# Attention scores over all 128 partitions: q's two parts stacked, k's parts copied to both halves by transfers

## The chip, the cores and the metric

The kernel runs on one core of one Trainium2 chip. The metric is device time in microseconds (us) of one execution. The engines are named as in the profile: PE (TensorE matmul), PEld (its weight load), DVE (VectorE), ACT (ScalarE), POOL (GpSimd) and SP (SyncE).

## What is computed

Two blocks of a small transformer, one after the other, on 512 tokens of width 1024, all in float32. The first block has two attentions of 8 heads with head width 64: a windowed one in which four query heads share a key head (call it a), and a neighbourhood one in which every head has keys of its own (b). The second block is run for two layers, each with one sliding-window attention (c) between two feed-forward parts. What matters here are the scores, cut from the reference:

```python
# a: windowed_gqa, 128 queries against up to 3 blocks of 128 keys
sc = jnp.einsum('bqkgd,bskd->bkgqs', qi, ki).astype(jnp.float32) * scale
# b: neighborhood_attn
sc = jnp.einsum('bchd,brckhd->bhcrk', qr, kn).astype(jnp.float32) * scale
# c: sliding_window_attention, 128 queries against 2 blocks of 128 keys
scores = jnp.einsum("bnqkgd,bnskd->bnkgqs", qb, k_band).astype(jnp.float32) * scale
p = jnp.exp(scores - m)
```

`d` is the head width of 64, so a score sums over 64 products. The rest of each block is matrix products of the whole 512 x 1024 activation with weights of 234 MB in all.

## The kernel before

Every float32 matrix is split into an upper part (the value rounded to the short float32 that PE multiplies in one pass, type fp32r) and a lower part (what is left over). A product is three matmuls: upper times upper, upper times lower, lower times upper (`Tile.mm`, L450 to L452, 128 x 512 each). ACT makes the upper part and DVE the lower one, for weights (`split_item`, L376 and L378, tiles `wh` and `wl`) as for activations (`split_act`, L553 and L554). Split activations live in 52 slots, tiles `r`, that are taken and given back (`take`, `give`). SP loads the weights from a stream in program order.

A tile of q or k holds two heads, one on partitions 0 to 63 and one on partitions 64 to 127. When its product is done, `ev_split` takes it out of PSUM: DVE multiplies by the norm's factor (tile `evs`), ACT writes the upper part into one slot, DVE the lower part into another. A head's q and k then lie on the same 64 partitions.

`run_attention` goes through steps of 128 queries and two heads: 32 steps in the first block (16 of a, tiles `sa`, then 16 of b, tiles `sb`) and 16 in each layer of the second (tiles `sc`). Four steps share a q tile; in b each four steps have a k tile of their own, in a and c one k tile serves all. A step `s` is four functions: `qk` (scores on PE at L717, then bias and row maximum on DVE), `soft` (exponential on ACT, division on DVE), `tr` (PE transposes the probabilities, `pt`) and `pv_` (times v, `yp`). `tr` runs one step behind `qk` in the first block and two steps behind in the second, `pv_` another step behind. Between these, fillers keep PE at work: other projections of the same block, in an order written out by hand (`FILL_AB`, `FILL_C`), each cut in parts of `STEP` = 2 row blocks, paced so that they last through all steps. Before step 0, `2 * head` such parts are done. The q and k tiles of later steps are fillers too; the last k tile of b, `("kb", 3)`, is followed by `("vb", 3)`, and then comes step 12 of b, which needs both. Queues run in order on each engine, so a `qk` that waits holds up all of PE behind it.

The head of each attention is `linear2`: q's and k's products side by side, then v's, in the midst of which q and k are taken out.

POOL does little: some additions at the very start, twelve loads of b's bias (L992, tile `bb`) and eight reloads of x (L1037). An `ft` tile is one of five buffers for passing values such as `evs`.

Of the kernel before, what the change touches and what calls it, by code (L numbers as in the profile page):

```python
# [15 lines left out]
P = 128  # L16
# [215 lines left out]
def two_blocks(ctx, tc, plan, xT, wstream, vecs, sinks, rpb_g, dists, masks, outT):  # L232
# [464 lines left out]
    def make_attention(kind, q, k, v, y, bias_of, sink_idx, band):  # L697
# [6 lines left out]
        def qk(s):  # L704
            c, i = divmod(s, 4)
            ks = keys(i)
            n = P * len(ks)
            sp = bank(f"s{kind}{s}", True).rearrange("p (g k) -> p g k", g=2)
            qh, ql = q(c)
            kh, kl = k(c)  # L710
            w = max(n, 2 * P)
            sl = slice(P * ks[0], P * ks[0] + w)
            for g in range(2):
                r = slice(HD * g, HD * g + HD)
                qs = slice(P * i, P * i + P)
                for j, (a, b) in enumerate(((qh, kh), (qh, kl), (ql, kh))):
                    nc.tensor.matmul(sp[:, g, :w], a[r, qs], b[r, sl], start=(j == 0), stop=(j == 2))  # L717
            bt = bias_of(c, i)
            t = big("t", f"t{kind}{s}").rearrange("p (g k) -> p g k", g=2)
            mx = sm_p.tile([P, 8], F32, tag="mx", name=f"mx{kind}{s}")  # L720
            for g in range(2):
                nc.vector.tensor_tensor_reduce(
                    out=t[:, g, :n], in0=sp[:, g, :n], in1=bt[:, g, :n], scale=1.0, scalar=-3.0e38,
                    op0=ALU.add, op1=ALU.max, accum_out=mx[:, g:g + 1])
            nm = mx[:, 2:4]
            if sink_idx is None:
                nc.vector.tensor_scalar(nm, mx[:, 0:2], -1.0, None, ALU.mult)
            else:
                sv = snk[:, sink_idx, :].rearrange("p (g c) -> p c g", g=2)[:, c, :]
                nsv = nsnk[:, sink_idx, :].rearrange("p (g c) -> p c g", g=2)[:, c, :]  # L730
                nc.vector.scalar_tensor_tensor(nm, mx[:, 0:2], -1.0, nsv, ALU.mult, ALU.min)
                nc.vector.tensor_tensor(mx[:, 4:6], nm, sv, ALU.add)
            state[s] = (t, mx, n, ks)
# [50 lines left out]

        return qk, soft, tr, pv_

    def run_attention(steps, fillers, needs, head=1, late=False):

        n = len(steps)
        lag = LAG2 if late else LAG1  # L790
        slots = n + lag + 1
        hold = [] if late else [50, 51]
        assert all(i in free for i in hold)
        free[:] = [i for i in free if i not in hold]
        total = sum(f[1] for f in fillers)
        parts, have, cost = [], set(), [0.0]
        queue = list(fillers)

        def fill():
            if not parts:  # L800
                key, c, make = queue.pop(0)
                fs = make()
                parts.extend((key if i == len(fs) - 1 else None, c / len(fs), f) for i, f in enumerate(fs))
            key, c, f = parts.pop(0)
            cost[0] += c
            f()
            have.add(key)

        def fill_to(share, slack):
            while (queue or parts) and cost[0] < total * share - slack:  # L810
                fill()

        for _ in range(2 * head):
            fill()
        total -= cost[0]
        cost[0] = 0.0

        for s in range(slots):
            if s < n:
                while not set(needs(s)) <= have:  # L820
                    fill()
                if any(key[-len(k):] == k for k in needs(s) for key, _ in evacs):
                    evacuate()
                steps[s][0](steps[s][4])
            evacuate()
            fill_to((s + MID) / slots, SLACK[0])
            if s > lag:
                k = s - lag - 1
                steps[k][3](steps[k][4])
            if lag <= s < n + lag:  # L830
                steps[s - lag][2](steps[s - lag][4])
            if s < n:
                rest = steps[s][1](steps[s][4])
                split_to(st["next"] + 2)
                rest()
            fill_to((s + 1) / slots, SLACK[1])
        assert not queue and not parts
        evacuate()
        flush()
        give(hold)  # L840
# [15 lines left out]
            inv.rearrange("p (r c) -> p r c", r=8), ALU.mult, ALU.mult)  # L856
        return t

    def ev_split(ids, scale=1.0, turn=scaled):
        def f(ps):  # L860
            split_act(turn(ps, "evs", scale), slot[ids[0]], slot[ids[1]])
        return f

    def ev_v(ids, turn=scaled):
# [68 lines left out]
    nc.vector.tensor_tensor(gfg, vcols(("norm_final", None)), vcols(("ffn1_norm_2", 0)), ALU.mult)  # L933
    nc.vector.tensor_scalar(nsnk, snk, -1.0, None, ALU.mult)
    qa, ya, yb, qb, kb, vb = {0: take(2)}, {}, {}, {}, {}, {}
    ka, va = take(2), take(2)
    linear2(MIX1_HEAD, xop, [ev_split(qa[0], QS), ev_split(ka), ev_v(va)], ar, KC, make_inv)
    ya_done = []

    def ev_ga(n):  # L940
# [17 lines left out]
    def fill(key):  # L958
        def make():
            if key[0] == "ga":  # L960
                return halves(key, xop, ev_ga(key[1]))
            if key[0] == "gb":
                return halves(key, xop, ev_gb(key[1]))
            if key[0] == "pa":
                assert ya_done
                return halves(key, [pair_of(ya[k]) for k in range(4)], ev_pa(key[1]))
            ids = take(2)
            {"qa": qa, "qb": qb, "kb": kb, "vb": vb}[key[0]][key[1]] = ids
            ev = {"qa": lambda: ev_split(ids, QS), "qb": lambda: ev_split(ids, QS, scaled_by_columns),
                  "kb": lambda: ev_split(ids, 1.0, scaled_by_columns), "vb": lambda: ev_v(ids, scaled_by_columns)}  # L970
            return halves(key, xop, ev[key[0]]())
        return (key, 0.5 if key[0] == "pa" else 1.0, make)

# [21 lines left out]
    def rpb_bias(c, i):  # L995
# [9 lines left out]
        if i != 2:  # L1005
            nv = (c, v + 1) if v < 2 else (c + 1, 0)
            if nv[0] < 4 and nv not in bias_cache:
                rpb_load(*nv)
        return bt[:, :, P:] if i == 0 else bt

    f_a = make_attention("a", ids_pair(qa), lambda c: pair_of(ka), lambda c: pair_of(va),
                         y_plain(ya, lambda c: qa[c] + (ka + va if c == 3 else []), ya_done),
                         alibi("a", 0, 384), 0, (-1, 0, 1))
    f_b = make_attention("b", ids_pair(qb), ids_pair(kb), ids_pair(vb),
                         y_plain(yb, lambda c: qb[c] + kb[c] + vb[c]), rpb_bias, None, (-1, 0, 1))

    def needs_ab(s):
# [291 lines left out]

    def mix2(l, before):  # L1310
        qs, ys, tmp = {0: take(2)}, {}, {}
        ks, vs = take(2), take(2)
        linear2([(l,) + k for k in MIX2_HEAD], xop, [ev_split(qs[0], QS), ev_split(ks), ev_v(vs)], ar, 1, make_inv)
        cs = [take(2, late=True) for _ in range(4)]
        nc.vector.tensor_tensor(inv2, inv, inv, ALU.mult)

# [22 lines left out]
        def fl(key):  # L1339
            def make():  # L1340
                if key[0] == "q":
                    qs[key[1]] = take(2)
                    return halves((l,) + key, xop, ev_split(qs[key[1]], QS))
                return halves((l,) + key, xop, ev_conv(*key))
            return (key, 1.0, make)

        f_c = make_attention(f"c{l}", ids_pair(qs), lambda c: pair_of(ks), lambda c: pair_of(vs),
                             y_plain(ys, lambda c: qs[c] + (ks + vs if c == 3 else [])),
                             alibi(f"c{l}", 384, 256), 1 + l, (-1, 0))
        run_attention([(*f_c, s) for s in range(16)], [fl(k) for k in FILL_C],  # L1350
# [80 lines left out]
```

## Time and profile before

| what | value |
|---|---|
| median of 3 runs | 2463.43 us (2463.13 to 2463.51) |
| the profiled execution: device time | 2464.76 us |
| its span on the core | 2463.0 us |
| granted PE clock, mean | 0.996 |
| PE busy | 2436.1 us, 99% |
| DVE busy | 1960.7 us, 80% |
| ACT busy | 1261.0 us, 51% |
| POOL busy | 24.6 us, 1% |

The profiled execution took 1.33 us more than the median of the runs. An engine's busy time is the time in which at least one of its instructions is under way; matmuls overlap each other, so a share of 99% says that PE had nothing to wait for, not that it could do no more.

### The profile page before, as it was taken

To read this page: it belongs to the slowest core of one execution; us is meant where nothing else is said; L and a number is where in the kernel's file an instruction comes from. 1 tells how busy PE (TensorE), PEld (TensorE's weight loads), DVE (VectorE), ACT (ScalarE), POOL (GpSimd) and SP (SyncE) were. 2 spreads that over 40 slices of the span, in tenths; PEclk is the share of its full clock that TensorE was granted. 3 is DMA by queue.
4 is the path that set the end of the run, shared out by engine and by line. 5 is a ranking of instruction groups with operands and counts; after the bars stand their busy time and mean duration, and the time that the engine had idled before them with its cause. 6 is when DMAs were issued, how large, how long until landed. Compare 5 with 4: busy or idle time off the path is not lost.

```text
span 2463.0 us, 39488 instructions
## 1 busy us (share of the span) xinstructions
PE 2436.1 (99%) x15098; PEld 2167.0 (88%) x15098; DVE 1960.7 (80%) x3943; ACT 1261.0 (51%) x2744; POOL 24.6 (1%) x37
## 2 busy tenths in 40 slices
PE   8999999999999999999999999999999999999998
PEld 6888888999879999988899999899999878999997
DVE  7778678877679878768798888898887687988885
ACT  5554355544455545544565445665445455654454
POOL 2000000000000000000000000000000000000000
PEclk9999999999999999999999999999999999999999
DMA  4222432233322332332223323323333322233332
GB/s 161 69 92 88 118 114 82 94 101 100 106 85 91 101 115 88 114 95 69 84 80 103 107 99 101 102 93 112 98 104 106 102 69 77 75 107 108 106 94 79
DMA packets 73901, 239.45 MB, mean 97 GB/s; under 512 B 8320, under 2 KB 10384, under 8 KB 73712
## 3 DMA queue, kind: packets, MB, share of 16 engines
q1 hardware_dynamic: 70496, 228.10, 29.0%
q0 software_dynamic: 1776, 7.27, 1.0%
q8 instruction: 118, 1.93, 0.3%
q10 hardware_dynamic: 1440, 1.57, 0.2%
q14 instruction: 71, 0.58, 0.1%
HBM read 234.81 MB, written 2.10 MB: 96 GB/s over the span
## 4 chain that ended last, share of the span: by engine, by line
PE 93%; DVE 5%; ACT 1%; issue 0%; DMA 0%; SPq 0%; DVEq 0%; ACTq 0%
PE X L1084 7%; PE X L1083 7%; PE X L1082 7%; PE YZ L1082 5%; PE YZ L1083 5%; PE YZ L1084 5%; PE mlp_D L451 2%; PE mlp_D L450 2%; PE mlp_D L452 2%; PE 0, 'ffn2'_D L450 2%; PE 1, 'ffn1'_D L450 2%; PE 0, 'ffn1'_D L450 2%; PE 0, 'ffn1'_D L451 2%; PE 0, 'ffn2'_D L451 2%; PE 1, 'ffn1'_D L451 2%; PE 0, 'ffn1'_D L452 2%
## 5 line engine op out<-in xcount | busy, mean ns | idle before, releaser
L378 DVE TENSOR_TENSOR wl<-raw,wh 128x512 fp32r<-128x512 f32 (+2 forms) x890 | 531.7, 609 | 98.3 <-ACT wh L376 91.4
L376 ACT CAST wh<-raw 128x512 fp32r<-128x512 f32 (+2 forms) x890 | 469.6, 555 | 8.4 <-DMA raw<-in_w 2.6
L1082 PE MATMUL X<-r,wh 128*128 128x256 f32 x1568 | 445.2, 284 | 3.8 <-ACT g L1088 3.6
L1084 PE MATMUL X<-r,wl 128*128 128x256 f32 x1568 | 444.0, 283 | 0.0
L1083 PE MATMUL X<-r,wh 128*128 128x256 f32 x1568 | 443.9, 283 | 0.0
L376 ACT CAST wh<-s 128x512 fp32r<-128x512 f32 x392 | 242.7, 620 | 224.6 <-DVE s L355 219.2
L1082 PE MATMUL YZ<-r,wh 128*128 128x256 f32 x1176 | 334.4, 284 | 0.8 <-ACT u L1094 0.8
L1083 PE MATMUL YZ<-r,wh 128*128 128x256 f32 x1176 | 333.3, 283 | 0.0
L1084 PE MATMUL YZ<-r,wl 128*128 128x256 f32 x1176 | 333.2, 283 | 0.0
L378 DVE TENSOR_TENSOR wl<-s,wh 128x512 fp32r<-128x512 f32 x392 | 268.8, 686 | 69.5 <-ACT wh L376 67.6
L1082 PEld LDWEIGHTS X<-r,wh 128*128 128x128 f32 x1568 | 300.1, 191 | 15.2 <-ACT g L1088 4.0
L1083 PEld LDWEIGHTS X<-r,wh 128*128 128x128 f32 x1568 | 300.1, 191 | 10.3 <-issue 1.2
L1084 PEld LDWEIGHTS X<-r,wl 128*128 128x128 f32 x1568 | 300.2, 191 | 0.0
L1082 PEld LDWEIGHTS YZ<-r,wh 128*128 128x128 f32 x1176 | 226.3, 192 | 1.6 <-ACT u L1094 1.4
L1083 PEld LDWEIGHTS YZ<-r,wh 128*128 128x128 f32 x1176 | 226.3, 192 | 0.2 <-issue 0.2
L1084 PEld LDWEIGHTS YZ<-r,wl 128*128 128x128 f32 x1176 | 226.3, 192 | 0.0
L1096 ACT COPY g<-X 128x256 f32<-128x256 f32 x98 | 36.5, 372 | 141.6 <-PE X L1084 141.5
L1097 DVE TENSOR_TENSOR u<-u,g 128x256 f32<-128x256 f32 x98 | 41.6, 424 | 75.8 <-ACT g L1096 75.8
L450 PE MATMUL mlp_D<-r,wh 128*128 128x512 f32 x256 | 100.1, 391 | 0.0
L451 PE MATMUL mlp_D<-r,wh 128*128 128x512 f32 x256 | 100.1, 391 | 0.0
L452 PE MATMUL mlp_D<-r,wl 128*128 128x512 f32 x256 | 99.6, 389 | 0.0
L1092 ACT COPY u<-X 128x256 f32<-128x256 f32 x98 | 36.5, 373 | 101.0 <-PE X L1084 101.0
(429 smaller groups left out, 5258.9 us busy)
## 6 DMA issues: line engine op xcount, KB each, us to landing
raw<-in_w SPq DMA_DIRECT2D x320, 512.0 KB, 3.7
raw<-in_w SPq DMA_DIRECT2D x64, 384.0 KB, 3.5
raw<-in_w SPq DMA_DIRECT2D x32, 448.0 KB, 3.5
raw<-in_w SPq DMA_DIRECT2D x32, 320.0 KB, 2.9
raw<-in_w SPq DMA_DIRECT2D x28, 256.0 KB, 2.6
bb<-in_rpb POOLq DMA_DIRECT2D x12, 384.0 KB, 3.3
xt<-in_x POOLq DMA_DIRECT2D x8, 256.0 KB, 2.9
xt<-in_x SPq DMA_DIRECT2D x1, 1024.0 KB, 12.7
```

What stands on the lines that cost most here:

```text
L376: nc.scalar.copy(h[:, :w], src)
L378: nc.vector.tensor_tensor(lo[:, :w], src, h[:, :w].bitcast(F32), ALU.subtract)
L450: nc.tensor.matmul(self.ps, h[:, c], hx, start=(self.n == 1), stop=False)
L451: nc.tensor.matmul(self.ps, h[:, c], lx, start=False, stop=False)
L452: nc.tensor.matmul(self.ps, lo[:, c], hx, start=False, stop=end)
L1082: nc.tensor.matmul(out, h[:, c], hx, start=first, stop=False, skip_group_check=skip)
L1083: nc.tensor.matmul(out, h[:, c], lx, start=False, stop=False, skip_group_check=skip)
L1084: nc.tensor.matmul(out, l[:, c], hx, start=False, stop=(k == 3), skip_group_check=skip)
L1092: nc.scalar.copy(u[:, lo], out)
L1096: nc.scalar.copy(g[:, hi], out)
L1097: nc.vector.tensor_tensor(u[:, hi], u[:, hi], g[:, hi], ALU.add)
```

## The change

`ev_split` is replaced by `ev_q` and `ev_k`. Both take the product out of PSUM as before (DVE, then ACT for the upper part into an `ft` tile `evh`, then DVE for the lower part, now in place in `evs`). Then POOL issues copies from SBUF to SBUF of 64 partitions x 512 columns each. For q there are four: each head gets a slot of its own, with the upper part on one half of the partitions and the lower part on the other. For k there are eight: each head gets two slots, one with its upper part on both halves, one with its lower part on both halves. `qk` then does two matmuls for a head instead of three, each over 128 partitions: the stacked q against the doubled upper part of k, and against the doubled lower part. This also adds the product of lower and lower part, which was left out before. k takes four slots instead of two, and `head` goes from 1 to 2.

```diff
             sp = bank(f"s{kind}{s}", True).rearrange("p (g k) -> p g k", g=2)
-            qh, ql = q(c)
-            kh, kl = k(c)
             w = max(n, 2 * P)
             sl = slice(P * ks[0], P * ks[0] + w)
             for g in range(2):
-                r = slice(HD * g, HD * g + HD)
-                qs = slice(P * i, P * i + P)
-                for j, (a, b) in enumerate(((qh, kh), (qh, kl), (ql, kh))):
-                    nc.tensor.matmul(sp[:, g, :w], a[r, qs], b[r, sl], start=(j == 0), stop=(j == 2))
+                qg, kg = slot[q(c)[g]], k(c)[2 * g:2 * g + 2]
+                for j in range(2):
+                    nc.tensor.matmul(sp[:, g, :w], qg[:, P * i:P * i + P], slot[kg[j]][:, sl], start=(j == 0), stop=(j == 1))
...
-    def run_attention(steps, fillers, needs, head=1, late=False):
+    def run_attention(steps, fillers, needs, head=2, late=False):
...
-    def ev_split(ids, scale=1.0, turn=scaled):
+    def parts(ps, scale, turn):
+
+        t = turn(ps, "evs", scale)
+        h = ft("evh")
+        split_act(t, h.bitcast(F32R), t)
+        return h, t
+
+    def move(i, half, src, head):
+        nc.gpsimd.dma_start(slot[i].bitcast(F32)[HD * half:HD * half + HD, :], src[HD * head:HD * head + HD, :])
+
+    def ev_q(ids, turn=scaled):
+
         def f(ps):
-            split_act(turn(ps, "evs", scale), slot[ids[0]], slot[ids[1]])
+            h, lo = parts(ps, QS, turn)
+            for src, flip in ((h, 0), (lo, 1)):
+                for g in range(2):
+                    move(ids[g], g ^ flip, src, g)
+        return f
+
+    def ev_k(ids, turn=scaled):
+
+        def f(ps):
+            for j, src in enumerate(parts(ps, 1.0, turn)):
+                for g in range(2):
+                    for half in range(2):
+                        move(ids[2 * g + j], half, src, g)
         return f
...
-    ka, va = take(2), take(2)
-    linear2(MIX1_HEAD, xop, [ev_split(qa[0], QS), ev_split(ka), ev_v(va)], ar, KC, make_inv)
+    ka, va = take(4), take(2)
+    linear2(MIX1_HEAD, xop, [ev_q(qa[0]), ev_k(ka), ev_v(va)], ar, KC, make_inv)
...
-        ks, vs = take(2), take(2)
-        linear2([(l,) + k for k in MIX2_HEAD], xop, [ev_split(qs[0], QS), ev_split(ks), ev_v(vs)], ar, 1, make_inv)
+        ks, vs = take(4), take(2)
+        linear2([(l,) + k for k in MIX2_HEAD], xop, [ev_q(qs[0]), ev_k(ks), ev_v(vs)], ar, 1, make_inv)
```

Where it moves instructions, first on PE at step 12 of b (its score tile is `sb_2425` before and `sb_2454` after; `vb` is the filler ahead of it). Before:

```order
L451 MATMUL vb_2384<-r_103,wh_2212 128x512
L452 MATMUL vb_2384<-r_102,wl_2213 128x512
L717 MATMUL sb_2425<-r_106,r_112 128x256
L717 MATMUL sb_2425<-r_107,r_112 128x256
L717 MATMUL sb_2425<-r_106,r_113 128x256
```

The same three follow once more, for the head on the other 64 partitions. Now:

```order
L451 MATMUL vb_2404<-r_103,wh_2231 128x512
L452 MATMUL vb_2404<-r_102,wl_2232 128x512
L714 MATMUL sb_2454<-r_114,r_112 128x256
L714 MATMUL sb_2454<-r_115,r_112 128x256
L714 MATMUL sb_2454<-r_118,r_113 128x256
L714 MATMUL sb_2454<-r_119,r_113 128x256
L775 MATMUL yb_2468<-r_138,r_110 128x256
```

Six matmuls became four, at the same place behind `vb`; the fourth reads the slot that k's last two copies fill (`r_119`).

Second, POOL's queue over the same stretch of the program. Before it holds bias loads only:

```order
L992 DMA bb_2040<-in_rpb 128x768
L992 DMA bb_2136<-in_rpb 128x768
L992 DMA bb_2203<-in_rpb 128x768
L992 DMA bb_2333<-in_rpb 128x768
L992 DMA bb_2434<-in_rpb 128x768
```

Now the copies stand among them (`x2` is two of a kind in a row; the four `r_112` and `r_113` are q's for steps 12 to 15 of b, the eight behind `bb_2363` are k's for the same steps):

```order
L1012 DMA bb_2222<-in_rpb 128x768
L864 DMA r_112<-evh 64x512
L864 DMA r_113<-evh 64x512
L864 DMA r_112<-evs 64x512
L864 DMA r_113<-evs 64x512
L1012 DMA bb_2363<-in_rpb 128x768
L864 DMA r_114<-evh 64x512 x2
L864 DMA r_118<-evh 64x512 x2
L864 DMA r_115<-evs 64x512 x2
L864 DMA r_119<-evs 64x512 x2
L1012 DMA bb_2461<-in_rpb 128x768
```

Over the whole program POOL gets 64 copies for 16 q tiles and 56 for 7 k tiles.

Third, PE at the first step of a, in the head of the first block. Before, the scores come when half of the filler `qa` is done:

```order
L450 MATMUL qa_373<-r_94,wh_253 128x512
L451 MATMUL qa_373<-r_95,wh_253 128x512
L452 MATMUL qa_373<-r_94,wl_254 128x512
L717 MATMUL sa_392<-r_106,r_104 128x256
L717 MATMUL sa_392<-r_107,r_104 128x256
L717 MATMUL sa_392<-r_106,r_105 128x256
```

Now, with `head` = 2, they come when all of it is done, twelve matmuls and v's four transposes (`vtr`) later:

```order
L452 MATMUL qa_387<-r_102,wl_317 128x512
L891 MATMUL vtr<-ident,evv 128x128 x4
L714 MATMUL sa_429<-r_106,r_104 128x256
L714 MATMUL sa_429<-r_107,r_104 128x256
L714 MATMUL sa_429<-r_108,r_105 128x256
L714 MATMUL sa_429<-r_109,r_105 128x256
L450 MATMUL qa_452<-r_88,wh_322 128x512
```

The first step of c in each layer moves in the same way.

## Rows read from the trace of the kernel before

**Rows 1.** The page: busy time by engine, share of the span, instructions.

```profile
PE 2436.1 (99%) x15098; PEld 2167.0 (88%) x15098; DVE 1960.7 (80%) x3943; ACT 1261.0 (51%) x2744; POOL 24.6 (1%) x37
```

**Rows 2.** Busy time by stretch, around c's first layer: PE, PEld, DVE, ACT, POOL.

```profile
1075.00:1150.00 75.00, 75.00 (x401) 59.32 (x400) 57.52 (x175) 36.33 (x103) 0.00 (x0) 1.00 0.22 66
```

**Rows 3.** Line 717, the scores of b: duration ns min/median/max, first and last start, forms.

```profile
L717 PE MATMUL sb<-r,r x96: 271/333/442, 142.0 to 249.1; 64*128 64x256 f32 x48, 64*128 64x384 f32 x48
```

**Rows 4.** PE in order of time, two score blocks: start us, us, operation, count.

```profile
149.50 0.39 PE L452 MATMUL kb<-r,wl 128*128 128x512 f32 x1
...
150.88 0.39 PE L451 MATMUL kb<-r,wh 128*128 128x512 f32 x1
...
1101.59 0.39 PE L452 MATMUL 0_ch<-r,wl 128*128 128x512 f32 x1
1101.91 0.62 PE L717 MATMUL sc<-r,r 64*128 64x256 f32 x6
1102.47 0.50 PE L450 MATMUL 0_ch<-r,wh 128*128 128x512 f32 x1
1102.81 0.40 PE L451 MATMUL 0_ch<-r,wh 128*128 128x512 f32 x1
```

**Rows 5.** PE in order of time, matmuls over 128 partitions, then transposes.

```profile
1109.45 0.39 PE L452 MATMUL 0_q<-r,wl 128*128 128x512 f32 x1
1109.67 0.88 PE L778 MATMUL yc<-r,r 128*128 128x256 f32 x6
1110.39 0.60 PE L758 MATMUL ptc<-ident,tc 128*128 128x128 f32 x4
1110.75 0.48 PE L450 MATMUL 0_q<-r,wh 128*128 128x512 f32 x1
```

**Rows 6.** PE in order of time, what runs between 1101.80 and 1102.00.

```profile
1101.91 0.39 PE L717 MATMUL sc<-r,r 64*128 64x256 f32 x2
```

**Rows 7.** POOL issuing one load; DMA issues: KB each, median us to landing.

```profile
222.06 0.54 POOL L992 DMA_DIRECT2D bb<-in_rpb  x1 [5.92 <-DVE mxb L727]
...
bb<-in_rpb POOLq DMA_DIRECT2D x12, 384.0 KB, 3.3
xt<-in_x POOLq DMA_DIRECT2D x8, 256.0 KB, 2.9
```

**Rows 8.** ACT and PE in order of time around step 12 of b.

```profile
229.19 0.62 ACT L553 CAST r<-evs 128x512 fp32r<-128x512 f32 x1 [1.99 <-DVE evs L854]
...
229.06 0.39 PE L451 MATMUL vb<-r,wh 128*128 128x512 f32 x1
229.29 0.39 PE L452 MATMUL vb<-r,wl 128*128 128x512 f32 x1
...
231.14 0.39 PE L778 MATMUL yb<-r,r 128*128 128x256 f32 x1
```

**Rows 9.** ACT and PE in order of time around step 8 of b.

```profile
194.73 0.62 ACT L553 CAST r<-evs 128x512 fp32r<-128x512 f32 x1 [3.65 <-DVE evs L854]
...
200.45 0.39 PE L452 MATMUL vb<-r,wl 128*128 128x512 f32 x1
```

**Rows 10.** ACT and PE in order of time around the first step of c.

```profile
1083.82 0.62 ACT L553 CAST r<-evs 128x512 fp32r<-128x512 f32 x1 [1.36 <-DVE evs L846]
...
1086.24 0.39 PE L452 MATMUL 0_q<-r,wl 128*128 128x512 f32 x1
```

**Rows 11.** Busy time by stretch; behind POOL stands the granted clock.

```profile
710.73:714.17 3.44, 0.00 (x0) 0.00 (x0) 3.15 (x6) 3.02 (x6) 0.00 (x0) 1.00 0.83 297
714.17:720.99 6.82, 6.22 (x15) 4.87 (x16) 6.44 (x11) 5.33 (x12) 0.00 (x0) 0.50 0.01 4
751.30:754.18 2.88, 0.04 (x2) 0.00 (x1) 2.88 (x7) 1.46 (x4) 0.00 (x0) 1.00 0.00 0
755.13:758.54 3.41, 3.41 (x19) 3.41 (x17) 3.41 (x7) 0.92 (x4) 0.00 (x0) 0.50 0.02 5
```

**Rows 12.** DVE's waits in the first stage of c: us in total, times, longest.

```profile
DVE tc L722 <- PE sc L717: 0.2, 1, 0.2
```

More of the change, by code (lines that the diff above doesn't have):

```diff
@@ L966, in make @@
                 return halves(key, [pair_of(ya[k]) for k in range(4)], ev_pa(key[1]))
-            ids = take(2)
+            ids = take(4 if key[0] == "kb" else 2)
             {"qa": qa, "qb": qb, "kb": kb, "vb": vb}[key[0]][key[1]] = ids
-            ev = {"qa": lambda: ev_split(ids, QS), "qb": lambda: ev_split(ids, QS, scaled_by_columns),
-                  "kb": lambda: ev_split(ids, 1.0, scaled_by_columns), "vb": lambda: ev_v(ids, scaled_by_columns)}
+            ev = {"qa": lambda: ev_q(ids), "qb": lambda: ev_q(ids, scaled_by_columns),
+                  "kb": lambda: ev_k(ids, scaled_by_columns), "vb": lambda: ev_v(ids, scaled_by_columns)}
             return halves(key, xop, ev[key[0]]())
@@ L1009, in rpb_bias @@
         return bt[:, :, P:] if i == 0 else bt
-    f_a = make_attention("a", ids_pair(qa), lambda c: pair_of(ka), lambda c: pair_of(va),
+    f_a = make_attention("a", qa.get, lambda c: ka, lambda c: pair_of(va),
                          y_plain(ya, lambda c: qa[c] + (ka + va if c == 3 else []), ya_done),
                          alibi("a", 0, 384), 0, (-1, 0, 1))
-    f_b = make_attention("b", ids_pair(qb), ids_pair(kb), ids_pair(vb),
+    f_b = make_attention("b", qb.get, kb.get, ids_pair(vb),
                          y_plain(yb, lambda c: qb[c] + kb[c] + vb[c]), rpb_bias, None, (-1, 0, 1))
@@ L1342, in make @@
                     qs[key[1]] = take(2)
-                    return halves((l,) + key, xop, ev_split(qs[key[1]], QS))
+                    return halves((l,) + key, xop, ev_q(qs[key[1]]))
                 return halves((l,) + key, xop, ev_conv(*key))
             return (key, 1.0, make)
-        f_c = make_attention(f"c{l}", ids_pair(qs), lambda c: pair_of(ks), lambda c: pair_of(vs),
+        f_c = make_attention(f"c{l}", qs.get, lambda c: ks, lambda c: pair_of(vs),
                              y_plain(ys, lambda c: qs[c] + (ks + vs if c == 3 else [])),
```

## The prediction

> **What bounds the kernel now.** First the page: PE is busy 99% of the span, DVE 80% [rows 1]. The reader is to see that a matmul saved where PE never waits is time saved, and that any wait put in front of a matmul is time lost. Then the stretch with the first c attention: PE 75.00 of 75.00 us, DVE 57.52 [rows 2]; nothing makes PE wait there. In the attentions of the first block the one wait of PE worth a line is at step 12 of b (below). So the question has two sides: what a score block costs PE now and would cost with four matmuls, and when the copies of q and k have landed against the place of the first score matmul in PE's queue.
>
> **What the scores cost now.** Neighbouring 128 x 512 matmuls start 0.23 us apart (229.06 to 229.29) [rows 8]. Around a score block of 256 columns, the last matmul ahead starts at 1101.59 and the second behind at 1102.81: 1.22 us, of which two spacings (0.46) belong to the neighbours, so the six matmuls cost 0.76 [rows 4]. With 384 columns it is 149.50 to 150.88, 1.38 - 0.46 = 0.92 [rows 4]. This 0.76 has two pieces. Six matmuls over 64 partitions run in pairs: between 1101.80 and 1102.00 two of them are under way, with the first start at 1101.91 [rows 6], and all six together take 0.62, less than six over 128 partitions, which take 0.88 [rows 4, 5]. And there are edges: the block starts 0.32 behind the matmul ahead of it instead of 0.23, and the first matmul behind it is followed after 0.34 instead of 0.23 [rows 4]: 0.09 + 0.11. A block of the same width over 128 partitions has no such edge at its front: 1109.45 to 1109.67 is 0.22 [rows 5].
>
> **What they would cost.** Six matmuls of 128 partitions x 256 columns take 1109.67 to 1110.39, 0.12 each [rows 5], so four take 0.48. For 384 columns no row shows one; between 0.12 (256) and 0.23 (512) halfway gives 0.175, four of them 0.70. Bounds for four: 0.48 and 0.92. Savings: 0.28 per 256-block and 0.22 per 384-block. Half of b's 96 score matmuls have 256 columns, half 384 [rows 3], which is 8 steps each; a has the same keys per step, and c's 32 steps all have 256. So 48 x 0.28 = 13.4 and 16 x 0.22 = 3.5: **a gain of 16.9 us**. Only a third of the matmuls goes, and nearly none of their streaming time: most of the gain is the edges.
>
> A page of the Trainium skill speaks against the change here: TensorEngine Tiling (Array Packing), Tiling Modes, Key Properties, says that tiles of the array work independently, so that weight loads and matmuls of different tiles run side by side. The pairs [rows 6] agree. By that rule alone, six half-height matmuls cost three passes and four full-height ones cost four, and 64 steps would lose one pass each. The same list says that a change of tiling mode drains the array; the edges [rows 4] would be that, and by it the sum stays as above.
>
> **The copies.** POOL needs 0.54 us for each DMA it issues; from issue to landing a load of 384 KB takes 3.3 us and one of 256 KB 2.9 [rows 7], so I carry the step of 0.4 on to the 128 KB of a copy: 2.5. The floor is 2.1, with that step taken twice off the smaller row (2.9 - 2 x 0.4); the ceiling 3.3. Eight copies in a row: the last is issued 7 x 0.54 = 3.8 after the first, and lands 6.3 after k's upper part is ready. Before, the scores could start when DVE had written the lower part, some 0.7 after that. The evacuations themselves (DVE, ACT, DVE) keep their instructions and cost the same. Where more than 6.3 us of PE work lie between, the copies cost nothing; that covers steps 4, 8 and 12 of a and steps 0 and 4 of b, whose tiles are fillers done many microseconds ahead. Steps 4, 8 and 12 of c need a new q tile alone, with four copies (3 x 0.54 + 2.5 = 4.1 to wait), and I count nothing for them either. Five places have less:
>
> *Step 12 of b.* k's upper part is ready at 229.19 + 0.62 = 229.81, the last copy lands at 236.1. PE could start the block at 229.29 + 0.23 = 229.52 [rows 8]; its fourth matmul, which reads the last copy, would start 0.36 later. It starts at 236.1 and the block ends at 236.2, 6.7 after 229.52. Before, the next work (yb) starts at 231.14, 1.62 after 229.52 [rows 8], because even now this block waits a little. The sum above counted 0.76 to 0.48 here; so the extra loss is (6.7 - 0.48) - (1.62 - 0.76) = **5.4**. Behind these matmuls stand v's products of step 10, the transposes of step 11 and filler `pa`, all ready: nothing of it can pass. POOL's next DMA, the bias of step 13, is issued at 234.1 and lands at 237.4, before step 13's scores (about 239), so it adds no wait of its own.
>
> *The clock.* PE would stand nearly idle for some 6 us at that place. Twice in this trace it stood idle: 3.44 us with no matmul, after which the granted clock was 0.50 (1.2 GHz) for 6.82 us; and 2.88 us, after which it was 0.50 for 3.41 us [rows 11]. At half the clock about half of that time is lost: 3.4 or 1.7. No row shows a shorter drop after so long a pause; I take **2.4**, with 0 and 3.4 as bounds.
>
> *Step 8 of b.* Ready at 194.73 + 0.62 = 195.35, landed at 201.6. PE's place: 200.45 + 0.23 = 200.68 [rows 9], less the 0.28 saved at step 7, plus 0.36 for the fourth matmul: 200.8. **0.9** late.
>
> *The first step of each attention* (a, and c twice). In c, k's upper part is ready at 1083.82 + 0.62 = 1084.44; q's four copies are issued before that. The last copy lands at 1090.7. The matmul ahead of the scores starts at 1086.24 [rows 10]; with `head` = 2 twelve more (2.76) and four transposes (1110.39 to 1110.75, 0.36 [rows 5]) come first, so the fourth score matmul has its place at 1086.24 + 0.23 + 2.76 + 0.36 + 0.36 = 1089.95. 0.8 late; the head of a has the same instructions in the same order. Three times: **2.4**. With `head` left at 1 it would be 3.9 each.
>
> **DVE.** It has 57.52 us of work in 75 of c [rows 2], the rest mostly waits on ACT in the middle of its own chains; for PE's scores it waited 0.2 us in the whole stage [rows 12]. Sixteen steps shorter by 0.28 take 4.5 us from a stage in which DVE has few pauses that belong to PE. The weight splits ahead and the one to two steps between scores and transposes cover some of it. Bounds 0 and 4.5 per stage; I take 1 each, **2.0**. The first block is longer for the same number of score matmuls and I take nothing there. Reuse of `evs` and `evh` makes DVE wait for old copies; with five `ft` buffers those left microseconds earlier: nothing.
>
> **Sum.** -16.9 + 5.4 + 2.4 + 0.9 + 2.4 + 2.0 = -3.8 us against the profiled execution's own 2464.76, which gives 2461.0; the median of the runs is 1.33 below the profiled one, so **2459.6 us** against 2463.43.
>
> **Rivals.**
> *Waits stay small* (2453). The copies land in 2.1, the clock doesn't fall and DVE follows: 0.4 less at five places (2.0), the 2.4 gone, the 2.0 gone: 3.8 + 6.4 = 10.2 us faster; with the 384-blocks at their floor of 0.48 another 16 x 0.22 = 3.5, 2450. For it: nothing measured here is a copy from SBUF to SBUF. Against it: rows 11, and eight copies behind each other share DMA engines with the weight stream.
> *The edges stay* (2473). If the 0.09 + 0.11 belong to something other than the 64-partition form, a block costs 0.68 instead of 0.48 and the gain is 16.9 - 64 x 0.2 = 4.1, against 13.1 of costs: 9.0 slower. It decides from an edge of 0.06 per block up, in the sense that above it no gain is left. Against it: the edgeless front in rows 5. This is what the skill's tiling rule makes of it if nothing is drained.
> *POOL is slow* (2485). If issuing takes twice 0.54 beside a busy DVE, each string of eight ends 3.8 later and each head (twelve copies) about 6: 2 x 3.8 + 3 x 6 = 25.6 more. For it speaks a page: SBUF — State Buffer, SBUF: two separate sides, warns that GpSimd can't write descriptors while DVE runs in a mode that takes both ports. Against it: 0.54 in the midst of b, where DVE is at work [rows 7].
> *DVE becomes the bound in c* (2467): 4.5 twice instead of 1 twice, 7 more. For it: the small rest in [rows 2]; against it: no pause of DVE there belongs to PE but 0.2 [rows 12].
>
> **Chances.** This forecast, 2455 to 2463: 0.60 (0.29 of it faster). Small waits: 0.14. Edges: 0.11. POOL: 0.08. DVE: 0.07. About 0.2% (4.9 us) is what a measurement can tell from no change: 2458.5 to 2468.4. Faster 0.29 + 0.14 = 0.43; same 0.31 + 0.07 = 0.38; slower 0.19. The range reaches from the small waits with their floor to the edges, 2450 to 2473, and leaves out POOL's 0.08 and some of both ends.
>
> **What would show it.** Right: score blocks of four matmuls about 0.12 apart, and 0.23 on both sides; PE idle some 5 to 6 us ahead of step 12 of b with a copy as releaser, about 1 us at step 8 and at each first step, nothing elsewhere; half clock behind step 12; POOL copies 0.54 apart. Wrong: an edge around the new blocks, copies further apart or landing over 3.3 us after issue, PE waiting on DVE inside c, or a wait at a step whose tiles I called early.

## The result, and the profile of the changed kernel

The changed kernel took 2495.60 us (median of 4 runs, 2494.75 to 2495.93), the kernel before beside it 2463.47. The ratio is 1.0129, with a 95% interval from 1.0112 to 1.0147: **32.1 us slower**, where 3.8 faster was forecast and 2450 to 2473 given as the range. The profiled execution has a span of 2492.9 us against 2463.0.

The score blocks did what was forecast. PE in order of time around one block of 256 columns (read as [rows 4]):

```profile
1142.96 0.40 PE L452 MATMUL 0_cb<-r,wl 128*128 128x512 f32 x1
1143.19 0.63 PE L714 MATMUL sc<-r,r 128*128 128x256 f32 x4
1143.66 0.40 PE L450 MATMUL 0_cb<-r,wh 128*128 128x512 f32 x1
1143.89 0.40 PE L451 MATMUL 0_cb<-r,wh 128*128 128x512 f32 x1
```

The block starts 0.23 behind the matmul ahead of it and the next pair stands 0.23 apart: both edges are gone. From 1142.96 to 1143.89 it is 0.93, less two spacings 0.47, where [rows 4] gave 0.76. The "drain" of the Trainium skill (TensorEngine Tiling (Array Packing), Tiling Modes, Key Properties) agrees with that. The independent tiles of the same list in the Trainium skill, by which this would have lost, are the smaller effect here.

What was lost stands in PE's waits, the whole execution (line waited for: us in total, times, longest). Before, no line of the attentions in this list was above 0.3 us.

```profile
PE sc L714 <- DMA r<-evs: 7.3, 4, 3.0
PE sb L714 <- DMA r<-evs: 6.1, 4, 3.5
PE vtr L891 <- DVE evv L851: 5.7, 2, 5.2
...
PE sb L714 <- DMA r<-evh: 3.8, 1, 3.8
...
PE sa L714 <- DMA r<-evs: 3.1, 1, 3.1
PE sa L714 <- DMA r<-evh: 2.4, 1, 2.4
PE yc L775 <- DVE r L554: 2.1, 2, 1.0
```

PE waited 22.7 us for copies (7.3 + 6.1 + 3.8 + 3.1 + 2.4), at the five places that the prediction named, which gave them 8.7. It also waited 5.2 at a place that the prediction did not name (v's transposes in b) and 1.0 in each c. Behind six of these waits the clock was halved (busy time by stretch: PE, PEld, DVE, ACT, POOL, granted clock; before, there were such stretches only outside the attentions, two of them in [rows 11]):

```profile
40.05:46.87 6.82, 4.56 (x12) 3.68 (x13) 2.58 (x9) 1.50 (x3) 0.61 (x2) 0.50 0.03 10
169.75:176.58 6.83, 5.59 (x21) 5.13 (x22) 2.80 (x5) 2.46 (x6) 0.54 (x1) 0.50 0.51 155
217.54:220.95 3.41, 2.95 (x14) 2.98 (x15) 0.95 (x5) 0.00 (x0) 0.00 (x0) 0.50 0.31 123
251.67:258.50 6.83, 5.12 (x19) 4.65 (x20) 1.27 (x6) 0.94 (x3) 1.00 (x2) 0.50 0.51 170
1115.24:1122.07 6.83, 5.33 (x13) 4.17 (x14) 2.74 (x9) 2.42 (x3) 1.53 (x3) 0.50 0.15 35
1985.64:1989.06 3.42, 2.91 (x9) 2.22 (x8) 1.44 (x7) 0.54 (x2) 0.00 (x0) 0.50 0.01 1
```

PE worked 26.5 of these 34.1 us at 0.50 (1.2 GHz), so at most 13.2 were lost to the clock. Waits (22.7 + 5.2 + 2.1) and clock (up to 13.2) are up to 43; less the 17 gained that is up to 26, while the two profiled spans differ by 29.9. At least 4 us of the loss stand in none of these rows; the run with DVE relieved, below, bears on them.

Step 12 of b, ACT, PE and POOL in order of time (compare [rows 8]):

```profile
246.57 0.62 ACT L553 CAST evh<-evs 128x512 fp32r<-128x512 f32 x1 [2.00 <-DVE evs L851]
...
246.66 0.39 PE L452 MATMUL vb<-r,wl 128*128 128x512 f32 x1
250.84 0.36 PE L714 MATMUL sb<-r,r 128*128 128x256 f32 x1 [3.79 <-DMA r<-evh]
253.22 0.77 PE L714 MATMUL sb<-r,r 128*128 128x256 f32 x2 [2.02 <-DMA r<-evs]
...
254.50 2.12 PE L775 MATMUL yb<-r,r 128*128 128x256 f32 x9
...
247.49 2.07 POOL L864 DMA_DIRECT2D r<-evh  x4 [9.41 <-ACT evh L553]
249.55 2.05 POOL L864 DMA_DIRECT2D r<-evs  x4
```

The picture is the forecast one: k's upper part is ready at 247.19, eight copies go out 0.51 apart, and the block ends 7.6 behind its place (246.89 to 254.50; 6.7 was forecast).

Step 8 of b, ACT, then PE (compare [rows 9]): k's upper part is ready at 209.27, the scores have their place at 213.30, and the block ends 5.05 later.

```profile
208.65 0.62 ACT L553 CAST evh<-evs 128x512 fp32r<-128x512 f32 x1 [3.66 <-DVE evs L851]
...
213.30 0.28 PE L714 MATMUL sb<-r,r 128*128 128x256 f32 x1
...
218.35 1.06 PE L775 MATMUL yb<-r,r 128*128 128x256 f32 x4
```

The head of a is where it went otherwise. POOL, then PE:

```profile
29.46 1.06 POOL L864 DMA_DIRECT2D r<-evh  x2 [6.51 <-ACT evh L553]
30.52 1.03 POOL L864 DMA_DIRECT2D r<-evs  x2
31.54 2.05 POOL L864 DMA_DIRECT2D r<-evh  x4
36.29 2.14 POOL L864 DMA_DIRECT2D r<-evs  x4 [2.71 <-DMA r<-evh]
...
38.85 0.35 PE L714 MATMUL sa<-r,r 128*128 128x256 f32 x1 [2.41 <-DMA r<-evh]
42.31 1.19 PE L714 MATMUL sa<-r,r 128*128 128x256 f32 x3 [3.10 <-DMA r<-evs]
```

After eight copies POOL stood still for 2.71 us, until the first of them, issued at 29.46, had landed 6.3 us later. Two runs reported below bear this out: with `head` back at 1 and with k earlier the first copy landed after 4.5 and 3.9 us, POOL stood still for 0.93 and 0.33, and the ninth went out 0.5 after that landing, as here (the profile puts these two short waits down to DVE).

The heads of c differ from this. In the first layer the first copy landed after 2.2 us, and the ninth went out without a pause. In the second layer it also landed after 2.2 us, and POOL stood still before the ninth for 2.69 all the same; the profile names nothing that it waited for ("issue"), and no run explains it. ACT, POOL and PE in the first layer, then POOL in the second:

```profile
1106.96 0.62 ACT L553 CAST evh<-evs 128x512 fp32r<-128x512 f32 x1 [1.41 <-DVE evs L843]
1107.90 2.05 POOL L864 DMA_DIRECT2D r<-evh  x4
1117.50 0.55 PE L714 MATMUL sc<-r,r 128*128 128x256 f32 x1 [1.49 <-DMA r<-evs]
...
1981.98 2.10 POOL L864 DMA_DIRECT2D r<-evs  x4 [2.69 <-issue]
```

In a the copies also landed late. The times from issue to landing (min/median/max) are those of the copies issued in 29 to 34 us (a's head), 58 to 60.5 (a q tile alone), 209 to 213.6 (step 8 of b) and 247 to 251.5 (step 12 of b):

```profile
DMA to landing us min/median/max: 6.3/6.5/6.7
...
DMA to landing us min/median/max: 2.1/2.7/2.7
...
DMA to landing us min/median/max: 2.5/4.7/4.9
...
DMA to landing us min/median/max: 2.2/2.9/3.0
```

The two extremes differ in what else the DMA engines did (busy time by stretch; the last two columns are their busy share and GB/s, copies included):

```profile
29.00:34.00 5.00, 5.00 (x23) 4.13 (x22) 4.06 (x7) 2.35 (x5) 4.12 (x8) 1.00 0.98 281
...
58.00:60.50 2.50, 2.50 (x19) 2.29 (x18) 1.90 (x3) 1.06 (x3) 2.04 (x4) 1.00 0.51 139
```

The 2.5 us that the prediction carried is right for copies that have the DMA engines to themselves and 4 us short in the midst of the weight stream. The Trainium skill (DMA: Bandwidth & Descriptors, Queues, rings and completion order) says that each DMA engine goes round the queues that have work, packet by packet. The trace agrees as far as copies took 4.7 to 6.7 beside weight loads (in a's head, and the later ones at step 8), and 2.1 to 3.0 at the other two places. The heads of c are mixed: up to 6.0 in the first layer, but 2.2 to 3.0 in the second, where a weight load was issued among the copies too. No run took the weight loads away, so that cause of the late landing is read from the trace and not shown by an experiment.

The wait that nobody had forecast:

```profile
165.45 0.39 PE L452 MATMUL vb<-r,wl 128*128 128x512 f32 x1
170.99 1.11 PE L891 MATMUL vtr<-ident,evv 128*128 128x128 f32 x4 [5.15 <-DVE evv L851]
```

At a step whose number is a multiple of four, `pv_` first puts out every transpose of v that is pending (`evacuate` and `flush`). With `head` = 2 the filler `vb` ended right ahead of the `pv_` of step 0 of b; before, a whole filler, a score block and a product with v lay between (the last matmul of `vb` started at 160.78, `vtr` at 169.05). DVE came to `evv` at 169.87, 4.4 us after the last matmul of `vb` had started, and PE stood still.

### The profile page after: what moved, and what is told of

It reads as the page before. It is cut to its first block, busy times and chain, and to the rows that moved or that the text cites. A ratio compares the mean times of both kernels' runs of the same rounds, so it can differ in the third digit from the quotient of the medians.

```text
span 2492.9 us, 39528 instructions
## 1 busy us (share of the span) xinstructions
PE 2434.9 (98%) x14970; PEld 2186.5 (88%) x14970; DVE 1961.0 (79%) x3943; ACT 1260.9 (51%) x2744; POOL 86.8 (3%) x157
## 4 chain that ended last, share of the span: by engine, by line
PE 79%; DVE 12%; ACT 5%; issue 2%; DMA 2%; POOL 1%; SPq 0%; ACTq 0%; DVEq 0%; POOLq 0%
PE X L1104 7%; PE X L1102 7%; PE X L1103 7%; PE YZ L1102 5%; PE YZ L1104 5%; PE YZ L1103 5%; DVE wl L378 3%; PE mlp_D L451 2%; PE mlp_D L450 2%; PE mlp_D L452 2%; PE 0, 'ffn2'_D L450 2%; PE 1, 'ffn1'_D L450 2%; PE 0, 'ffn1'_D L450 2%; PE 0, 'ffn1'_D L451 2%; PE 1, 'ffn1'_D L451 2%
## 5 line engine op out<-in xcount | busy, mean ns | idle before, releaser
L864 POOL DMA_DIRECT2D r<-evh x60 | 31.0, 522 | 1842.7 <-ACT evh L553 1775.7
```

The source lines that it names most:

```text
L864: nc.gpsimd.dma_start(slot[i].bitcast(F32)[HD * half:HD * half + HD, :], src[HD * head:HD * head + HD, :])
```

## The experiments

Theory A, formed on the trace: four matmuls are worth what their blocks show; all of the loss is PE waiting at few places, for copies that have too little work ahead of them, for v's transposes that `head` = 2 moved, and for the clock behind each wait. Rivals: DVE becomes the bound (B); the transfers do harm by themselves (C); others as they came.

**The matmuls alone.** No copies, all four matmuls over 128 rows of tiles written in place:

```diff
-                qg, kg = slot[q(c)[g]], k(c)[2 * g:2 * g + 2]
+                qg, kg = slot[q(c)[g]], k(c)[0:2]
...
-            h, lo = parts(ps, QS, turn)
-            for src, flip in ((h, 0), (lo, 1)):
-                for g in range(2):
-                    move(ids[g], g ^ flip, src, g)
+            split_act(turn(ps, "evs", QS), slot[ids[0]], slot[ids[1]])
```

> Leaves out: q's and k's copies; both matmuls of a head take their 128 rows from tiles written in place, so the scores are other numbers (same shapes, same types, four matmuls per step), and head is 1 as before the change. Theory A (the four matmuls save what the score blocks show, and all that the change lost is waiting): 16.9 us below the kernel before, 2444 to 2449, with score blocks of 0.93 and 1.17 between the neighbours' starts and no idle time of PE above 0.5 us in the attentions. Rival B (DVE becomes the bound once scores are shorter): PE waits on DVE in both c stages, 4.5 us each, and the time is 2453 to 2457.

Measured: 2451.69 us, ratio 0.9951 (0.9936 to 0.9966), 11.6 below the kernel before: between the ranges of Theory A and rival B. PE's waits in the attentions are short, and all of them above 0.2 us are on DVE; the longest:

```profile
PE sb L714 <- DVE r L554: 1.1, 2, 0.8
...
PE pta L755 <- DVE ta L746: 1.0, 1, 1.0
```

**The copies alone.** Six matmuls as before, and the 120 copies into spare slots:

```diff
             split_act(turn(ps, "evs", scale), slot[ids[0]], slot[ids[1]])
+            extra = ids[2:]
+            for j in range(2):
+                src = slot[ids[j]].bitcast(F32)
+                for g in range(2):
+                    if turn is not None and scale != 1.0:
+                        move(extra[g % 1], g ^ j, src, g)
+                    else:
+                        for half in range(2):
+                            move(extra[(2 * g + j) % 2], half, src, g)
```

> The kernel before (six matmuls, head 1) with the same 120 copies issued by POOL, into slots that nobody reads. Theory A (a copy costs only where a score waits for it): within 3 us of the kernel before, 2461 to 2467. Rival C (the transfers do harm by themselves: they delay the weights, the bias loads or DVE): 10 us or more above it, with PE waiting on weights or bias.

Measured: 2473.93 us, ratio 1.0043 (1.0026 to 1.0060): 10.7 above, so Theory A as it stood missed. 5.3 of it are one wait, at step 13 of b, and up to 3.4 the half clock behind it (243.68 to 250.51):

```profile
238.56 1.03 POOL L860 DMA_DIRECT2D r<-r  x2 [2.38 <-DMA r<-r]
239.57 1.09 POOL L1004 DMA_DIRECT2D bb<-in_rpb  x2
243.28 0.56 DVE L722 CUSTOM_DVE_ANT_0 tb<-sb,bb 128x384 f32<-128x384 f32 x1 [6.25 <-DMA bb<-in_rpb]
244.38 1.11 PE L758 MATMUL ptb<-ident,tb 128*128 128x128 f32 x4 [5.33 <-DVE mxb L722]
```

Here two copies share a half of a spare slot, so the later one waits on POOL until the earlier has landed; a bias load stands behind them in POOL's queue, DVE waits for the bias and PE for DVE. That is this edit's own arrangement, but the way is real: a copy that waits on POOL holds up the bias loads. In the changed kernel no wait of PE has this cause.

**`head` back at 1.**

```diff
-    def run_attention(steps, fillers, needs, head=2, late=False):
+    def run_attention(steps, fillers, needs, head=1, late=False):
```

> The changed kernel with head back at 1. Theory A (the wait of 5.15 us for v's transposes in b, and the half clock behind it, are there because head = 2 moved the fillers against the steps): that wait goes (5.2 + 3.4 less), and the three first steps come some 2.7 us earlier and wait that much longer (8.1 more): 2490 to 2500. Rival D (that wait comes from the copies in front of the bias loads in POOL's queue): it stays, and the time is 2500 to 2506.

Measured: 2491.39 us, 1.0113 (1.0098 to 1.0128). The wait of 5.15 for v's transposes is gone from the list, so `head` = 2 made it, and the first steps wait longer, both as Theory A had it:

```profile
PE sc L714 <- DMA r<-evs: 9.3, 4, 4.4
...
PE sa L714 <- DMA r<-evh: 3.7, 1, 3.7
```

**Half the copies.** The own half is written in place (shown for k):

```diff
+            for g in range(2):
+                r = slice(HD * g, HD * g + HD)
+                nc.scalar.copy(slot[ids[2 * g]][r, :], t[r, :])
+                move(ids[2 * g], 1 - g, slot[ids[2 * g]].bitcast(F32), g)
+            for g in range(2):
+                r = slice(HD * g, HD * g + HD)
+                nc.vector.tensor_tensor(slot[ids[2 * g + 1]][r, :], t[r, :], slot[ids[2 * g]].bitcast(F32)[r, :], ALU.subtract)
+                move(ids[2 * g + 1], 1 - g, slot[ids[2 * g + 1]].bitcast(F32), g)
```

> The changed kernel (head 2), but each head's own half is written in place by ACT and DVE, and only the other half is copied: 60 copies instead of 120, a string of four behind k instead of eight, two behind q instead of four. Theory A (the string, 0.51 us a copy, makes the scores late): 3.1 less at each of the three first steps and 2.0 less at steps 8 and 12 of b, 13 in all, and half of the clock's loss with it: 2472 to 2484. Rival E (the landing time beside the weights sets it, whatever the number): under 5 us gained, 2490 or more.

Measured: 2485.67 us, 1.0091 (1.0076 to 1.0106), 1.7 above the range of A. The waits for copies fell from 22.7 to 5.4 (5.1 in b and 0.3 in c), so a shorter string removes them. It shortens three things at once (the issue, POOL's pause after eight copies, and the landing, which for k's copies at the heads was now 2.2 to 3.2), and this run does not part them. Waits on DVE took their place:

```profile
PE vtr L893 <- DVE evv L851: 6.5, 2, 6.0
PE pta L755 <- DVE ta L746: 5.1, 7, 2.1
PE sb L714 <- DMA r<-r: 5.1, 4, 3.3
```

**k earlier.** The changed kernel with another order of fillers:

```diff
-           ("qb", 0), ("kb", 0), ("ga", 5), ("ga", 6), ("qb", 1), ("kb", 1), ("vb", 1), ("ga", 7), ("pa", 0),
-           ("qb", 2), ("kb", 2), ("pa", 2), ("vb", 2), ("pa", 1), ("qb", 3), ("kb", 3), ("vb", 3), ("pa", 4),
+           ("qb", 0), ("kb", 0), ("ga", 5), ("ga", 6), ("kb", 1), ("qb", 1), ("vb", 1), ("ga", 7), ("kb", 2),
+           ("qb", 2), ("pa", 0), ("pa", 2), ("vb", 2), ("kb", 3), ("qb", 3), ("pa", 1), ("vb", 3), ("pa", 4),
```

> The changed kernel with another order of fillers in the first block: each k tile of b from the second on comes before its q tile, and the last two a filler or more earlier still, so that about 18 us of PE work instead of 7 and 10 lie between a k tile's product and the scores that need it. Theory A (those two waits are the string of eight copies against too short a distance): the waits of PE at steps 8 and 12 of b (3.9 and 5.8 us) and the half clock behind them (1.7 and 3.4) go, 14.8 less: 2478 to 2484. Rival C (copies slow the block whatever their place): less than 5 gained, 2490 or more, with the waits moved to bias or DVE.

Measured: 2480.55 us, 1.0071 (1.0054 to 1.0087): 15.1 less than the changed kernel, as A had it. No wait for `sb` is left in the list; the heads' and v's are.

**PE kept at work in the waits.**

```diff
+            if (kind, s) in WARM or (kind[0], s) == ("c", 0):
+                for _ in range(36):
+                    nc.tensor.transpose(sp[:, 0, :P], ident, ident)
```

> The changed kernel with 36 transposes of the identity (about 3.3 us of PE work that nobody reads) just ahead of the scores at the five late places: step 0 of a, steps 8 and 12 of b, step 0 of each c. The waits for the copies stay as long as they are, only PE is not idle in them. Theory A (the half clock behind the waits comes from PE standing idle): the five stretches at 0.50 behind these places shrink or go, up to 13.6 less: 2482 to 2488. Rival F (the half clock has another cause, or the transposes only push work back): 2494 to 2500.

Measured: 2488.73 us, 1.0101 (1.0086 to 1.0116), 6.9 less than the changed kernel. All five stretches at half clock went, and the sixth, behind v's transposes in b, where no work had been put, stayed (167.64 to 174.47, at 0.50). At 1.00 stood, for one, the stretch over step 12 of b:

```profile
245.00:256.00 11.00, 8.50 (x58) 7.58 (x57) 4.29 (x14) 2.18 (x7) 4.39 (x9) 1.00 0.57 168
```

So it is PE's standing idle that halves the clock at these places, and 6.9 is a lower bound of its price there: the transposes took up to 4.1 us a place and at step 8 of b and in both c outlasted the wait.

**Halves by ACT.** As half the copies, with ACT in DVE's place:

```diff
+    def own(i, src, g):
+        r = slice(HD * g, HD * g + HD)
+        nc.scalar.copy(slot[i][r, :], src[r, :])
...
+            h, lo = parts(ps, QS, turn)
+            for g in range(2):
+                own(ids[g], h, g)
+                move(ids[g], 1 - g, lo, g)
```

> As the kernel with half of the copies (60, head 2), but ACT puts the own halves in place and DVE has the same instructions as in the changed kernel. Theory A (half the copies still lost 3.5 us per c stage because DVE had one more instruction for each q tile): PE's waits for v's products in c fall from 3.5 to 1 per stage and the waits for transposes in a shrink: 2478 to 2483. Rival G (ACT takes over as the late one): 2485 or more.

Measured: 2499.84 us, 1.0145 (1.0130 to 1.0160): rival G. DVE's waits for ACT's weight casts (`wl`) in 30 to 285 us are 17.1 here, against 2.6 in the changed kernel and 9.4 in the kernel before:

```profile
DVE wl L378 <- ACT wh L376: 17.1, 11, 2.5
```

**The same with k early and the second v tile of b one filler earlier** (`("kb", 1), ("vb", 1), ("qb", 1)`):

> Own halves by ACT, 60 copies, head 2, k tiles of b early, and the second v tile of b one filler earlier, so that its transposes are not due at once. Theory A (with every copy early enough the change is worth what the run without copies showed, 2451.7): 2452 to 2458, with no wait of PE over 1.5 us in the attentions and no half clock there. Rival C (the transfers cost something of their own): 2462 or more.

Measured: 2490.53 us, 1.0108 (1.0093 to 1.0123), with no half clock in the attentions and no wait for v's transposes over 0.4: the forecast waits were gone, and the time was not. Instead 19 waits of 0.3 to 2.2 us lie in the first block, mostly on DVE and ACT. With k early and all 120 copies the time was 2480.55, so work put on ACT costs here too. How ACT's work makes PE wait is not shown step by step.

**The old form for the first two steps.** The changed kernel's evacuations and its 120 copies; steps 0 and 1 of a and of each c take six matmuls from the copies' sources, now in slots, `head` is 1, k is early as above:

```diff
+            near = mine if s < 2 else []
             for g in range(2):
+                if near:
+                    r = slice(HD * g, HD * g + HD)
+                    qs = slice(P * i, P * i + P)
+                    (qh, ql), (kh, kl) = [pair_of(m) for m in near]
+                    for j, (a, b) in enumerate(((qh, kh), (qh, kl), (ql, kh))):
+                        nc.tensor.matmul(sp[:, g, :w], a[r, qs], b[r, sl], start=(j == 0), stop=(j == 2))
+                    continue
                 qg, kg = slot[q(c)[g]], k(c)[2 * g:2 * g + 2]
```

> The changed kernel's evacuations and 120 copies, but steps 0 and 1 of a and of each c take the old six matmuls from the undivided tiles (the copies' sources, four more slots until step 1), head is 1, and the first block has the order of fillers with the k tiles of b early. Theory A (each copy that is early enough costs nothing): 2452 to 2458, six steps at the old price (1.7 us) above the run without copies (2451.7), no wait of PE over 1.2 us in the attentions, no half clock there. Rival C (the transfers, or the buffers that they hold, cost something of their own): 2462 or more, with waits on DVE spread over many steps as in the run with ACT's halves.

Measured: 2454.64 us against 2462.91 beside it, ratio **0.9966 (0.9954 to 0.9978)**: 8.3 faster than the kernel before and 41 faster than the changed one, with the same 120 copies, as Theory A had it. No stretch at half clock is left in the attentions. PE's longest waits there:

```profile
PE sc L723 <- DMA r<-evs: 1.1, 3, 0.4
PE pta L767 <- DVE ta L758: 1.0, 1, 1.0
```

**Only c changed.** a and b in the old form and order (the line is shown against the kernel of the experiment before this one):

```diff
-            near = mine if s < 2 else []
+            near = [q(c), k(c)] if kind in "ab" else mine if s < 2 else []
```

> Only c is changed: a and b as before (tiles on 64 partitions, six matmuls, no copies, old order of fillers), c with four matmuls and copies, its steps 0 and 1 with the old six, head 1. Theory A: the run without copies gained 3.7 us in each c stage, less 0.3 for each of two old steps: 6.2 below the kernel before, 2456 to 2459. Rival C (copies beside c's DVE-bound chain cost what they save): 2462 to 2466.

Measured: 2458.10 us, 0.9979 (0.9971 to 0.9988): 4.8 below the kernel before, within Theory A's range. If the parts add up, a and b bring about 3.5 of the 8.3.

**DVE relieved.** The run without copies, without the division:

```diff
-                nc.vector.reciprocal(den[:, 2:4], den[:, 0:2])
-                for g in range(2):
-                    nc.vector.tensor_scalar(t[:, g, :n], t[:, g, :n], den[:, 2 + g:3 + g], None, ALU.mult)
+                return
```

> The run without copies (scores of other numbers, four matmuls, head 1), with the division of the probabilities by their sum left out too: three DVE instructions less per step (0.17 and two of 0.31 us in c). Theory A (the 16.9 us of the four matmuls come to 12 there because DVE's chain then makes PE wait a little at many steps): most of the missing 5 us comes back, 2445 to 2449. Rival H (the matmuls save less than their blocks show): 2450 to 2453, as before.

Measured: 2445.96 us, 0.9931 (0.9919 to 0.9944), 17.0 below the kernel before and 5.7 below the run without copies (5.4 when each is taken against the kernel before beside it), as Theory A had it. Its control, the kernel before with the same lines left out:

> The control to the run without copies and without the division: the kernel before (six matmuls, no copies), with the division of the probabilities by their sum left out. Theory A (before the change PE hardly waited on DVE, so that a lighter DVE is worth nothing there): within 2 us of the kernel before. Rival I (the division costs PE time in any form of the scores): 4 to 6 us less, and then the run without the division says nothing of the four matmuls.

Measured: 2463.08 us against 2463.45, 0.9998 (0.9989 to 1.0007). A lighter DVE is worth nothing before the change and 5.7 us once the scores are short.

## Why the prediction was wrong

| step of the prediction | forecast | measured |
|---|---|---|
| four matmuls for six | -16.9 | -17.0 (DVE relieved, against its control -17.1) |
| step 12 of b | +5.4 | +6.3: block ends 7.6 behind its place instead of 6.7 |
| step 8 of b | +0.9 | +4.6: 213.30 to 218.35, less 0.48 |
| first steps of a, c, c | +2.4 | +12.8 (waits 5.5 and 7.3) |
| clock | +2.4, one place | six stretches, at most 13.2; five of them at least 6.9 |
| v's transposes in b | 0 | +5.2 |
| DVE | +2.0, in c | +5.7 without copies |

**Right: the matmuls, and the places.** The gain came block by block and in the sum, and most of it is the edges of the 64-partition form (0.20 of the 0.29 in a block of 256 columns). The five places that the prediction named are also the only ones where PE waited for copies.

**Mis-sized: "the last is issued 3.8 after the first, and lands 6.3 after k's upper part is ready".** This holds at step 12 of b, where the copies took 2.2 to 3.0. At the heads the last copy lands 11.6 us (a), 9.8 and 9.3 (c) after k's upper part is ready. By the trace three things make the difference. q's four copies are still going out when k is ready, which the prediction had ruled out ("issued before that"): 0.3 at each head. POOL pauses before the ninth copy: 2.7 in a, nothing in c's first layer, 2.7 in its second. And the last copy lands in 5.0, 5.9 and 2.7 instead of 2.5. So in c's first layer k is ready at 1107.58 and the last score matmul starts at 1117.50, 9.9 later. No run removed one of the three alone.

The prediction named the sharing of DMA engines with the weight stream, but gave it no price: [rows 7] had only medians of single loads far apart, and of the rivals only "Waits stay small" changed the landing time, to less. The rival that came nearest in time, "POOL is slow" (2485), did so by another mechanism: the copies went out 0.51 to 0.52 apart even in 29 to 34 us, where DVE was busy for 4.06 of 5.00 us.

**Mis-sized: step 8.** The prediction took k's place against PE from the trace of before (5.3 us between 195.35 and 200.68). In the changed kernel k's cast ended at 209.27 and the scores' place was 213.30: 4.0. With landings of 4.7 to 4.9 for the last copies that makes 4.6 instead of 0.9.

**Failed: where the prediction costed `head` = 2.** It counted the twelve matmuls that `head` = 2 puts ahead of the first steps and not that every later filler moves against the steps. That moved `vb` next to the `flush` of step 0 of b: 5.2 us and a half clock. Putting `head` back removed it.

**Failed in its place, right in c: DVE.** The prediction took 1 us for each c and nothing for the first block. From the first q product to the first output product (`0_q` to `0_wo`) c's first layer took 125.9 us without copies and 124.9 with DVE relieved, so 1 was right; from a's v product to b's projection (`va` to `pb`) it is 237.6 against 234.2, where nothing was forecast.

**The clock** was costed at one place because one long wait was forecast. In the changed kernel it came behind six, so the cost grew with the number of waits.

By the runs, of the 36 us between forecast and result about 6 are steps 8 and 12 with their clock (15.1 measured by moving k, 8.7 forecast). Some 25 are the heads, v's transposes and the clock behind these: from the run with k early to the one with the old start 25.9 went, with 1.7 given back for six steps in the old form, 27.6 where 2.4 was forecast. Under 4 are DVE (5.7 against 2.0), if DVE costs with the copies what it cost without them.

## What to carry to other kernels

A transfer that replaces engine work has to be placed like a load: count the whole string in front of it in its queue and take its landing time from the busiest stretch in which it will run, not from quiet rows. Where the first use comes too soon, keep the old form for the first one or two steps and let the copies land behind them; here that, with k earlier and `head` back at 1, turned 32 us lost into 8 gained with the same copies. A parameter that shifts fillers shifts all of them: read the whole order behind it for places where a flush has nothing left ahead of it, and count a half clock behind each new long wait, as each of the six in the changed kernel's attentions had one.

## What the runs showed of the hardware

- Eight copies issued by POOL were under way at once in a's head; the ninth went out at 36.29 after a wait of 2.71 that ended with the landing of the first. Where the first landed sooner (after 4.5 and 3.9 us instead of 6.3), the wait was 0.93 and 0.33. The pause of 2.69 at the same place in c's second layer is not explained by this.
- A 128 KB copy from SBUF to SBUF landed 2.1 to 2.5 us after issue as the first of a string, 2.7 to 3.2 in the midst of one, and up to 6.7 beside weight loads; the bias loads in the same queue went from a median of 3.3 [rows 7] to 5.2.
- The granted clock stood at 0.50 behind six waits of the changed kernel; with work of no use put on PE in five of them it stayed at 1.00 there, and at 0.50 behind the sixth.
- ACT was busy for 124 of 230 us (30 to 260) in the run with its halves, 54%, and still four more copies per k tile and two per q tile left the kernel no faster than the changed one with 60 transfers fewer (2499.84 against 2495.60).
